# Spreading a norm weight by 128-row products, a reordered and fenced first stage, and tiles that start on multiples of 256 bytes

## The chip, the cores and the metric

The kernel runs on one core of one Trainium2 chip. The metric is the device time of one execution in microseconds (us), as the median of several runs. One execution was also recorded by the hardware profiler; its span runs from the first to the last instruction of the program.

## What is computed

One decoder layer on a sequence of 512 tokens with 1024 channels, all in 32-bit floats: a root-mean-square norm, one wide input projection, a gated linear recurrence (8 heads of 128, chunks of 32), causal multi-head attention with low-rank queries and keys (8 heads), a gated merge of the two branches, an output projection, a residual and a last norm. Cut to what matters:

```
h     = rms_norm(x, norm_g)                  # 512 x 1024
proj  = h @ w_in                             # 1024 x 7872 columns
hq, hf, hi, hz, cq, ckv, kr, mz, glog = split(proj)
y_a   = hgrn2_branch(hq, hf, hi, hz, ...)    # linear recurrence, silu gate
y_b   = mla_branch(cq, ckv, kr, mz, ...)     # causal attention, silu gate
gates = sigmoid(glog + b_gate)
x     = x + (gates[0] * (y_a @ w_proj_a) + gates[1] * (y_b @ w_proj_b)) @ w_out
out   = rms_norm(x, final_norm_g)
```

## The kernel before

Every large matrix product is made of three TensorE products. Each operand is split into a high part, which is the value rounded to the format fp32r, and a low part, which is the rest; `mm3` (L79 to L84) adds high by high (L82), high by low (L83) and low by high (L84) in one accumulator in PSUM. Weights come by DMA into one of three buffers `w_raw` of 128 x 1024 floats; `load_w` (L86 to L105; DMA at L100) casts them to `w_hi` on ScalarE (L103) and subtracts to get `w_lo` on VectorE (L104). There are four buffers of each.

**The first stage** (L145 to L302) norms the tokens, turns them so that channels lie on partitions (`hT`, a high and a low tile of 128 x 8 x 512), and makes the first 256 columns of the low-rank projection. It goes by four blocks of 128 tokens, t = 0 to 3. For each block: `squares` (L218) sums squares on ScalarE and takes the power -1/2 on GpSimd; `scaled` (L223) multiplies on VectorE the block by that and by the norm weight, which lies in two PSUM tiles `ng`, and writes `xn`; `turned` (L228) transposes eight pieces on TensorE (L233), copies them as `hT` high on ScalarE (L235) and subtracts to get `hT` low on VectorE (L236); `c_product` (L239) multiplies with the first two weight halves `c_raw` (L244), split by `c_split` (L212). Block 0 takes its own way to the root (L258 to L267), without GpSimd. The norm weight arrives as one row on one partition; two products with a row of ones (L254) spread it over 128 partitions. `idle_mm` (L207) makes products of a tile of zeros, whose result nobody reads.

**What sets the order.** The code of the first stage stands within `tc.manual_schedule` for TensorE, ScalarE and VectorE: their instructions keep the order in which they are written, among each other. All that is written after it is placed by a scheduler that goes by simulated times, and it may set later work in between. So products of the next 256 columns (L82 to L84 of `proj_tok`; their weights come through `load_cols`, L107) stand among those of the first stage, and so do the casts of their weights (L103). The SyncE queue issues nearly all DMAs in the written order.

**Where tiles lie.** Tiles get their places in SBUF one behind the other, from both ends of the memory. In the kernel before, tiles of 4 to 152 bytes a partition stand among the large ones. Added up, `w_raw`, `w_hi`, `w_lo`, `hT` and the output weights `wo` start 32 bytes past a multiple of 256 bytes; the two parts of `ya` and of `yb` (high and low of the branch outputs), `m` (merged) and `cT` (the low-rank rows, turned) start 224 bytes past one.

After the first stage come, in this order: the other columns of the low-rank projection, the recurrence in four pairs of heads with the input projection of each, attention head by head, the two merge projections, the output projection.

Of the kernel before, what the change touches and what calls it, by code (L numbers as in the profile page):

```python
# [38 lines left out]
def hybrid_layer(ctx: ExitStack, tc: tile.TileContext, a):  # L39
# [22 lines left out]
    class Pool:  # L62
# [5 lines left out]

        def tile(self, shape, dt, tag, bufs=1):
            return self.p.tile(shape, dt, tag=tag, name=tag, bufs=bufs)  # L70

        def close(self):
            self.cm.__exit__(None, None, None)

    hpool = Pool("hpool", "left")
    cpool = Pool("cpool", "right")
# [30 lines left out]
    def load_cols(mat, c0, w=256):  # L107

        v = mat[:, c0 : c0 + w].rearrange("(k p) c -> p k c", p=P)
        return [load_w(v[:, 4 * i : 4 * i + 4, :]) for i in range(2)]  # L110
# [13 lines left out]

    def proj_tok(mat, c0, w, lhs):

        halves = load_cols(mat, c0, w)
        ps = []
        for t2 in range(NT // 2):
            b = mm_tile()  # L130
            for t in range(2):
                tt = 2 * t2 + t
                for kk in range(KD):
                    mm3(b[:, t * 256 : t * 256 + w], lhs, halves[kk // 4],
                        (slice(None), kk, slice(tt * P, tt * P + P)), (slice(None), kk % 4),
                        kk == 0, kk == KD - 1)
            ps.append(b)
        return ps
# [6 lines left out]
    def power(out, x, mul, add, expo):  # L145

        nc.gpsimd.tensor_scalar(out, x, mul, add, op0=ALU.mult, op1=ALU.add)
        nc.gpsimd.tensor_tensor(out, out, expo, op=ALU.pow)
# [10 lines left out]
    ident = const.tile([P, P], F32, name="ident")  # L159
    neg_half = const.tile([P, 4], F32, name="neg_half")  # L160
    eps = const.tile([P, 1], F32, name="eps")
    nc.gpsimd.memset(eps[:], EPS)
    nc.gpsimd.memset(neg_half[:], -0.5)
    zero = st.tile([P, 512], BF16, "zero")
    ones = st.tile([1, P], F32, "ones")
    warm = st.tile([P, 1], F32, "warm")
    ng_row = st.tile([1, D], F32, "ng_row")
    x_sb = [st.tile([P, D], F32, "x", bufs=NT) for _ in range(NT)]
    hT = [hpool.tile([P, KD, S], F32R, f"hT{i}") for i in range(2)]
# [37 lines left out]
    def idle_mm(n):  # L207

        for _ in range(n):
            nc.tensor.matmul(idle[:], zero[:, :P], zero[:], start=True, stop=True)  # L210

    def c_split(kh, i, eng):  # L212

        hi, lo = c_hl[kh]
        nc.scalar.copy(hi[:, half[i]], c_raw[kh][:, half[i]])
        eng.tensor_tensor(lo[:, half[i]], c_raw[kh][:, half[i]], hi[:, half[i]].bitcast(F32), op=ALU.subtract)
# [31 lines left out]
    with tc.manual_schedule(engines={mybir.EngineType.PE, mybir.EngineType.Activation, mybir.EngineType.DVE}):  # L248
        nc.vector.memset(zero[:], 0.0)
        nc.vector.memset(ones[:], 1.0)  # L250
        nc.scalar.activation(warm[:], eps[:], AF.Sqrt)
        idle_mm(5)
        for n in range(2):
            nc.tensor.matmul(ng[n][:], ones[:], ng_row[:, half[n]], start=True, stop=True)  # L254
        idle_mm(3)

# [11 lines left out]
        scaled(0)  # L268
        c_split(0, 0, nc.vector)
        lo0 = turned(0, 0)  # L270
        lo0()
        c_split(0, 1, nc.vector)
        lo1 = turned(0, 1)
        c_product(0, 0, 0)
        c_product(0, 0, 1, (0, 1))
        c_product(0, 0, 2)
        c_product(0, 0, 1, (2, 3))
        lo1()
        squares(1)
        c_split(1, 0, nc.vector)  # L280
        c_split(1, 1, nc.gpsimd)
        squares(2)
# [5 lines left out]
        for t in range(1, NT):  # L288
            if t + 2 < NT:
                squares(t + 2)  # L290
            for kh in range(2):
                lo[kh]()
            if t + 1 < NT:
                scaled(t + 1)
            for kind in (0, 1, 2):
                c_product(t, 0, kind)
            if t + 1 < NT:
                nxt = [turned(t + 1, 0), turned(t + 1, 1)]
            for kind in (0, 2, 1):
                c_product(t, 1, kind)  # L300
            lo = nxt
    st.close()  # L302

# [33 lines left out]
    for c0, w in ((0, 256), (256, 256), (512, 192)):  # L337
        for t2, ps in enumerate(proj_tok(w_in, COL_C + c0, w, hT) if c0 else c_ps):
            nc.scalar.copy(c_sb[:, 2 * t2 : 2 * t2 + 2, c0 : c0 + w],
                           ps[:].rearrange("p (t c) -> p t c", t=2)[:, :, :w])  # L340
    css = cw.tile([P, 2, NT], F32, "css")
    for t in range(NT):
        for i, (o, n) in enumerate(((0, NQ), (NQ, NKV))):
            csq = cw.tile([P, NQ], F32, "csq", bufs=2)
            nc.scalar.activation(csq[:, :n], c_sb[:, t, o : o + n], AF.Square, accum_out=css[:, i, t : t + 1])
    power(css[:, 0, :], css[:, 0, :], 1.0 / NQ, EPS, neg_half[:])
    power(css[:, 1, :], css[:, 1, :], 1.0 / NKV, EPS, neg_half[:])
    kd = cw.tile([P, NT, 2, NR], F32, "kd")
# [126 lines left out]
    def hg_out(h, asb, st_, q128, v_sb):  # L475
# [8 lines left out]
        for i in range(NT):  # L484
            osq = W("osq", 1, (P, P))
            nc.scalar.activation(osq[:], ops[:, i * P : i * P + P], AF.Square, accum_out=ss[:, i : i + 1])
        power(ss[:], ss[:], 1.0 / P, 4 * EPS, neg_half[:])
        nc.vector.tensor_tensor(on[:].rearrange("p (g v) -> p g v", g=NT), ops[:].rearrange("p (g v) -> p g v", g=NT),
# [283 lines left out]
    m2p.close()  # L772
    mp.close()


# [36 lines left out]
```

## Time and profile before

| | us |
|---|---|
| median of 3 runs | 649.04 (648.63 to 650.54) |
| the profiled execution, its time | 648.64 |
| its span | 646.9 |
| TensorE busy (products) | 633.7, 98% |
| TensorE loading weights | 541.4, 84% |
| VectorE busy | 350.9, 54% |
| ScalarE busy | 240.7, 37% |
| GpSimd busy | 113.8, 18% |

PE is TensorE, PEld its weight loads, DVE is VectorE, ACT is ScalarE, POOL is GpSimd, SP is SyncE. A row of the timeline has the start, the duration, engine, line, operation, the tile written and the tiles read, and in brackets how long the engine was idle before it and what ended that. Products are pipelined and overlap, so the durations of single products don't add up; what one costs in a dense stretch is the distance from start to start. A row of the table of windows has the window, its length, busy time and count of instructions by engine, the granted TensorE clock as a share of full speed, the share of time in which the DMA engines were busy, and what they moved.

### The profile page before, as it was taken

How to read it: one execution, taken by the hardware profiler on the slowest of the kernel's cores; microseconds unless marked ns; L12 is line 12 of the kernel's file. 1: busy time of each engine (PE TensorE's matmuls, PEld its weight loads, DVE VectorE, ACT ScalarE, POOL GpSimd, SP SyncE). 2: the span in 40 equal slices, each digit the busy share in tenths (PEclk: the TensorE clock that was granted, in tenths of full speed). 3: DMA queues.
4: the chain of work that ended last, by engine and by line, in shares of the span. 5: the costliest groups of instructions: out<-in, count | busy, mean ns of one | idle time of the engine just before them, and what ended most of it. 6: DMA issues, size and time to landing. Idle time of an engine off the chain costs nothing.

```text
span 646.9 us, 9040 instructions
## 1 busy us (share of the span) xinstructions
PE 633.7 (98%) x3529; PEld 541.4 (84%) x3529; DVE 350.9 (54%) x543; ACT 240.7 (37%) x455; POOL 113.8 (18%) x212
## 2 busy tenths in 40 slices
PE   8799999999999999999999999999999999999995
PEld 4798988988898898888888988888888888888884
DVE  4533984676396377548485857845222342434244
ACT  5534422333223323435454546544122232323123
POOL 2104420331231032321223131000000010111011
PEclk9899999999999999999999999999999999999999
DMA  7433342142214113312424142133333323325403
GB/s 247 124 94 103 98 130 66 33 119 78 64 35 132 44 54 86 93 54 53 116 51 117 47 131 74 48 98 97 98 97 98 99 67 104 111 78 162 163 15 114
DMA packets 61944, 59.78 MB, mean 92 GB/s; under 512 B 5799, under 2 KB 57293, under 8 KB 61902
## 3 DMA queue, kind: packets, MB, share of 16 engines
q1 hardware_dynamic: 59628, 55.47, 29.1%
q10 hardware_dynamic: 2130, 3.22, 1.7%
q8 instruction: 27, 0.44, 0.3%
q0 software_dynamic: 144, 0.52, 0.3%
q14 instruction: 15, 0.12, 0.1%
HBM read 55.01 MB, written 2.10 MB: 88 GB/s over the span
## 4 chain that ended last, share of the span: by engine, by line
PE 96%; DMA 2%; SPq 0%; issue 0%; ACT 0%; DVE 0%; POOLq 0%; POOL 0%
PE mm_ps L82 26%; PE mm_ps L84 26%; PE mm_ps L83 26%; PE ax_ps L82 2%; PE ax_ps L83 2%; PE ax_ps L84 2%; PE ax_ps L604 2%; PE mm_ps L244 2%; DMA x<-x 1%; PE ax_ps L625 1%; PE ax_ps L461 1%; PE ax_ps L480 1%; PE ax_ps L482 1%; PE ax_ps L449 1%; DMA w_raw<-w_in 1%; PE ax_ps L469 1%
## 5 line engine op out<-in xcount | busy, mean ns | idle before, releaser
L104 DVE TENSOR_TENSOR w_lo<-w_raw,w_hi 128x1024 fp32r<-128x1024 f32 (+3 forms) x92 | 110.3, 1200 | 118.1 <-ACT w_hi L103 113.6
L103 ACT CAST w_hi<-w_raw 128x1024 fp32r<-128x1024 f32 (+3 forms) x92 | 89.8, 976 | 167.7 <-PE mm_ps L83 108.1
L82 PE MATMUL mm_ps<-hT,w_hi 128*128 128x512 f32 x384 | 151.5, 395 | 0.0
L84 PE MATMUL mm_ps<-hT,w_lo 128*128 128x512 f32 x384 | 150.5, 393 | 0.0
L83 PE MATMUL mm_ps<-hT,w_hi 128*128 128x512 f32 x384 | 150.0, 391 | 0.0
L84 PEld LDWEIGHTS mm_ps<-hT,w_lo 128*128 128x128 f32 x384 | 72.2, 188 | 14.9
L83 PEld LDWEIGHTS mm_ps<-hT,w_hi 128*128 128x128 f32 x384 | 72.2, 188 | 14.3
L82 PEld LDWEIGHTS mm_ps<-hT,w_hi 128*128 128x128 f32 x384 | 72.2, 188 | 14.2
L84 PE MATMUL mm_ps<-w_hi,hT 128*128 128x256 f32 (+1 forms) x192 | 54.3, 283 | 0.0
L82 PE MATMUL mm_ps<-w_hi,hT 128*128 128x256 f32 (+1 forms) x192 | 54.2, 282 | 0.0
L83 PE MATMUL mm_ps<-w_lo,hT 128*128 128x256 f32 (+1 forms) x192 | 54.1, 282 | 0.0
L715 POOL TENSOR_TENSOR ma<-ma,z 128x512 f32<-128x512 f32 x8 | 11.9, 1483 | 163.5 <-DVE z L714 163.5
L612 POOL TENSOR_SCALAR p<-p,sm 128x128 f32<-128x128 f32 (+3 forms) x32 | 20.3, 638 | 105.1 <-DVE sm L611 65.7
L82 PEld LDWEIGHTS mm_ps<-w_hi,hT 128*128 128x128 f32 x192 | 36.6, 191 | 0.2
L83 PEld LDWEIGHTS mm_ps<-w_lo,hT 128*128 128x128 f32 x192 | 36.6, 190 | 0.2
L84 PEld LDWEIGHTS mm_ps<-w_hi,hT 128*128 128x128 f32 x192 | 36.6, 190 | 0.0
L406 DVE RECIPROCAL tf<-pr 128x512 f32<-128x512 f32 x8 | 26.8, 3350 | 0.2
L610 ACT ACTIVATE p<-ax_ps,sm 128x128 f32<-128x128 f32 (+3 forms) x32 | 16.8, 528 | 23.2 <-DVE sm L609 22.9
L82 PE MATMUL mm_ps<-ya,w_hi 128*128 128x512 f32 x64 | 25.3, 396 | 0.0
L83 PE MATMUL mm_ps<-ya,w_hi 128*128 128x512 f32 x64 | 25.3, 395 | 0.0
L84 PE MATMUL mm_ps<-ya,w_lo 128*128 128x512 f32 x64 | 25.3, 395 | 0.0
L83 PE MATMUL mm_ps<-yb,w_hi 128*128 128x512 f32 x64 | 25.2, 394 | 0.0
(218 smaller groups left out, 1143.8 us busy)
## 6 DMA issues: line engine op xcount, KB each, us to landing
w_raw<-w_in SPq DMA_DIRECT2D x60, 512.0 KB, 4.0
w_raw<-w_proj_a SPq DMA_DIRECT2D x8, 512.0 KB, 3.7
w_raw<-w_proj_b SPq DMA_DIRECT2D x8, 512.0 KB, 3.5
wo_raw<-w_out SPq DMA_DIRECT2D x8, 512.0 KB, 3.3
w_raw<-w_ukv SPq DMA_DIRECT2D x16, 128.0 KB, 2.5
xr<-x SPq DMA_DIRECT2D x4, 512.0 KB, 6.5
x<-x SPq DMA_DIRECT2D x3, 512.0 KB, 8.9
w_raw<-w_uq SPq DMA_DIRECT2D x8, 192.0 KB, 2.8
```

The costliest lines, as they stand in the source:

```text
L82: nc.tensor.matmul(ps, lh[lsl], rh[rsl], start=start, stop=False)
L83: nc.tensor.matmul(ps, lh[lsl], rl[rsl], start=False, stop=False)
L84: nc.tensor.matmul(ps, ll[lsl], rh[rsl], start=False, stop=stop)
L103: nc.scalar.copy(hi[:, :o], raw[:, :o])
L104: (lo_eng or nc.vector).tensor_tensor(lo[:, :o], raw[:, :o], hi[:, :o].bitcast(F32), op=ALU.subtract)
L244: nc.tensor.matmul(ps, hT[l][:, 4 * kh + k, t * P : t * P + P], c_hl[kh][r][:, k * 256 : k * 256 + 256], start=kh == 0 and kind == 0 and k ...
L406: nc.vector.reciprocal(rp[:], pr[:])
L449: nc.tensor.matmul(sps[:, sl], kt_[:, sl], v_sb[:, i, (h % 2) * P : (h % 2) * P + P], start=True, stop=True)
L604: nc.tensor.matmul(sps[:, :n], qh[:, bl], kpe[x][:, :n], start=False, stop=x == 1)
L610: nc.scalar.activation(p[:, :n], sps[:, :n], AF.Exp, scale=SCALE, bias=sm[:, 1:2], accum_out=sm[:, 2:3])
L612: nc.gpsimd.tensor_scalar(p[:, :n], p[:, :n], sm[:, 3:4], 0.5, op0=ALU.mult, op1=ALU.mult)
L715: nc.gpsimd.tensor_tensor(ma[:, j], ma[:, j], g[:], op=ALU.add)
```

## The change

1. The norm weight. Two tiles `ng_r` of 128 x 1024 are cleared (a memset of a float tile and two casts, since fp32r is written by a cast); the first row of one gets the high part of the norm weight, that of the other the low part. Four fp32r products with a 128 x 128 tile of ones (high for both halves, then low) replace the two float products on one row.
2. The split of the first weights. Their high halves for block 0 are cast on VectorE in place of ScalarE, the low halves are made on VectorE and GpSimd; both transposes of block 0 stand ahead of its first product; the products of block 0 follow the order high-high, low-high, high-low without being split in two. The idle products become 6, 3, 3, 2 and 4 in number, from 5 and 3.
3. `tc.no_sync_barrier()` behind the first stage: nothing written after it is placed ahead of anything written before it. It makes no engine wait. The loads and splits of the next 256 columns are now written within the stage, after block 3 has been turned, and handed to `proj_tok`.
4. `Pool.tile` rounds each tile of these pools up to a multiple of 256 bytes a partition, a pool `edge` of 224 bytes is set at the right end, and `eps` and `neg_half` share a tile. Every tile of the pools, and each weight buffer, then starts on a multiple of 256 bytes.

```
         def tile(self, shape, dt, tag, bufs=1):
+            n = int(np.prod(shape[1:]))
+            q = 256 // mybir.dt.size(dt)
+            if n % q:
+                wide = self.p.tile([shape[0], -(-n // q) * q], dt, tag=tag, name=tag, bufs=bufs)[:, :n]
+                return wide if len(shape) == 2 else wide.rearrange("p (a b) -> p a b", a=shape[1])
             return self.p.tile(shape, dt, tag=tag, name=tag, bufs=bufs)
+    edge = Pool("edge", "right")
+    edge.p.tile([P, 56], F32, name="edge")
...
-    def proj_tok(mat, c0, w, lhs):
+    def proj_tok(mat, c0, w, lhs, halves=None):
-        halves = load_cols(mat, c0, w)
+        halves = halves or load_cols(mat, c0, w)
...
-    neg_half = const.tile([P, 4], F32, name="neg_half")
-    eps = const.tile([P, 1], F32, name="eps")
+    fixed = const.tile([P, 5], F32, name="fixed")
+    neg_half, eps = fixed[:, 0:4], fixed[:, 4:5]
-    ones = st.tile([1, P], F32, "ones")
+    ones = st.tile([P, P], F32, "ones")
+    ones_r = st.tile([P, P], F32R, "ones_r")
+    ng_z = st.tile([P, D], F32, "ng_z")
+    ng_r = [st.tile([P, D], F32R, f"ng_r{i}") for i in range(2)]
...
-    def c_split(kh, i, eng):
+    def c_hi(kh, i, eng):
+        eng(c_hl[kh][0][:, half[i]], c_raw[kh][:, half[i]])
+    def c_lo(kh, i, eng):
         hi, lo = c_hl[kh]
-        nc.scalar.copy(hi[:, half[i]], c_raw[kh][:, half[i]])
         eng.tensor_tensor(lo[:, half[i]], c_raw[kh][:, half[i]], hi[:, half[i]].bitcast(F32), op=ALU.subtract)
...
-        nc.scalar.activation(warm[:], eps[:], AF.Sqrt)
-        idle_mm(5)
-        for n in range(2):
-            nc.tensor.matmul(ng[n][:], ones[:], ng_row[:, half[n]], start=True, stop=True)
-        idle_mm(3)
+        nc.vector.tensor_copy(ones_r[:], ones[:])
+        nc.vector.memset(ng_z[:], 0.0)
+        for i in range(2):
+            nc.vector.tensor_copy(ng_r[i][:], ng_z[:])
+        nc.scalar.activation(warm[:], eps, AF.Sqrt)
+        idle_mm(6)
+        nc.vector.tensor_copy(ng_r[0][0:1], ng_row[:])
+        nc.vector.tensor_tensor(ng_r[1][0:1], ng_row[:], ng_r[0][0:1].bitcast(F32), op=ALU.subtract)
+        for x in range(2):
+            for n in range(2):
+                nc.tensor.matmul(ng[n][:], ones_r[:], ng_r[x][:, half[n]], start=x == 0, stop=x == 1)
+            idle_mm(3)
...
         scaled(0)
-        c_split(0, 0, nc.vector)
-        lo0 = turned(0, 0)
+        lo0, lo1 = turned(0, 0), turned(0, 1)
+        for i in range(2):
+            c_hi(0, i, nc.vector.tensor_copy)
         lo0()
-        c_split(0, 1, nc.vector)
-        lo1 = turned(0, 1)
+        c_lo(0, 0, nc.vector)
+        c_lo(0, 1, nc.gpsimd)
+        lo1()
+        idle_mm(2)
         c_product(0, 0, 0)
-        c_product(0, 0, 1, (0, 1))
         c_product(0, 0, 2)
-        c_product(0, 0, 1, (2, 3))
-        lo1()
+        c_product(0, 0, 1)
+        idle_mm(4)
         squares(1)
-        c_split(1, 0, nc.vector)
-        c_split(1, 1, nc.gpsimd)
+        for i in range(2):
+            c_hi(1, i, nc.scalar.copy)
+        c_lo(1, 0, nc.vector)
+        c_lo(1, 1, nc.gpsimd)
...
             if t + 1 < NT:
                 scaled(t + 1)
+            else:
+                c_second = load_cols(w_in, COL_C + 256)
...
             lo = nxt
+    tc.no_sync_barrier()
     st.close()
...
-        for t2, ps in enumerate(proj_tok(w_in, COL_C + c0, w, hT) if c0 else c_ps):
+        for t2, ps in enumerate(proj_tok(w_in, COL_C + c0, w, hT, c_second if c0 == 256 else None) if c0 else c_ps):
```

How the change moves instructions, at three places. In the rows below stand the line, the operation, the tile written, the tiles read, the size written, and xN where N alike follow each other; `hT` with the lower number is the high part. Lines of the kernel after are shifted: its L111 is L103 of before, its L247 L235, L256 L244, L90 to L92 are L82 to L84.

First, ScalarE from block 0's copies to those of block 2, before: two casts of `w_hi` at L103, which belong to the next 256 columns, stand ahead of the copies of `hT` for block 1.

```order
L215 CAST w_hi<-w_raw 128x512
L235 CAST hT_112<-ax_ps 128x4x128
L215 CAST w_hi<-w_raw 128x512
L235 CAST hT_112<-ax_ps 128x4x128
L220 ACTIVATE sq,rs<-x 128x1024
L215 CAST w_hi<-w_raw 128x512 x2
L220 ACTIVATE sq,rs<-x 128x1024
L103 CAST w_hi<-w_raw 128x1024 x2
L235 CAST hT_112<-ax_ps 128x4x128 x2
L220 ACTIVATE sq,rs<-x 128x1024
L235 CAST hT_112<-ax_ps 128x4x128 x2
```

The same place after:

```order
L247 CAST hT_119<-ax_ps 128x4x128 x2
L232 ACTIVATE sq,rs<-x 128x1024
L224 CAST w_hi<-w_raw 128x512 x2
L232 ACTIVATE sq,rs<-x 128x1024
L247 CAST hT_119<-ax_ps 128x4x128 x2
L232 ACTIVATE sq,rs<-x 128x1024
L247 CAST hT_119<-ax_ps 128x4x128 x4
L111 CAST w_hi<-w_raw 128x1024 x2
```

The two casts of the next columns have moved behind all copies of `hT`, and the two casts of the first weights for block 0 have left ScalarE.

Second, VectorE at the start, before, up to the first instruction that waits for a sum of squares:

```order
L249 MEMSET zero 128x256
L250 MEMSET ones 1x128
L261 TENSOR_SCALAR rsq_165<-rs 128x1
L263 TENSOR_SCALAR rsq_167<-rs,rsq_165 128x1
L264 TENSOR_SCALAR rsq_167<-rsq_167 128x1
```

And after:

```order
L261 MEMSET zero 128x256
L262 MEMSET ones 128x128
L263 CAST ones_r<-ones 128x128
L264 MEMSET ng_z 128x1024
L266 CAST ng_r_113<-ng_z 128x1024
L266 CAST ng_r_114<-ng_z 128x1024
L270 CAST ng_r_113<-ng_row 1x1024
L271 TENSOR_TENSOR ng_r_114<-ng_row,ng_r_113 1x1024
L281 TENSOR_SCALAR rsq_184<-rs 128x1
```

Six instructions now stand ahead of the root of block 0, two of which wait for the row of the norm weight. Further on, the two VectorE instructions on the masks (L317 and L318 before), which stood ahead of the low part of the second weight half, stand behind the whole stage.

Third, TensorE near the end of the stage, before: products of the next columns (L82 to L84) and the transpose of small parameters (L307) stand among the transposes and products of the stage.

```order
L233 MATMUL ax_ps<-ident,xn 128x128 x4
L82 MATMUL mm_ps<-w_hi,hT_112 128x256
L83 MATMUL mm_ps<-w_lo,hT_112 128x256
L233 MATMUL ax_ps<-ident,xn 128x128 x4
L244 MATMUL mm_ps<-w_hi,hT_112 128x256 x4
L244 MATMUL mm_ps<-w_hi,hT_113 128x256 x4
L244 MATMUL mm_ps<-w_lo,hT_112 128x256 x4
L307 MATMUL ax_ps<-ident,rows 128x38
L84 MATMUL mm_ps<-w_hi,hT_113 128x256
```

And after, where the stage ends:

```order
L256 MATMUL mm_ps<-w_hi,hT_119 128x256 x4
L256 MATMUL mm_ps<-w_hi,hT_120 128x256 x4
L256 MATMUL mm_ps<-w_lo,hT_119 128x256 x4
L334 MATMUL ax_ps<-ident,rows 128x38
L90 MATMUL mm_ps<-w_hi,hT_119 128x256
L91 MATMUL mm_ps<-w_lo,hT_119 128x256
L92 MATMUL mm_ps<-w_hi,hT_120 128x256
```

Nothing of the next columns is left within the stage: 24 products that stood between its transposes and products now follow it. From there on the order is that of before on every engine.

More of the change, by code (lines that the diff above doesn't have):

```diff
@@ L159, in hybrid_layer @@
     ident = const.tile([P, P], F32, name="ident")
-    neg_half = const.tile([P, 4], F32, name="neg_half")
-    eps = const.tile([P, 1], F32, name="eps")
-    nc.gpsimd.memset(eps[:], EPS)
-    nc.gpsimd.memset(neg_half[:], -0.5)
+    fixed = const.tile([P, 5], F32, name="fixed")
+    neg_half, eps = fixed[:, 0:4], fixed[:, 4:5]
+    nc.gpsimd.memset(eps, EPS)
+    nc.gpsimd.memset(neg_half, -0.5)
     zero = st.tile([P, 512], BF16, "zero")
-    ones = st.tile([1, P], F32, "ones")
+    ones = st.tile([P, P], F32, "ones")
+    ones_r = st.tile([P, P], F32R, "ones_r")
     warm = st.tile([P, 1], F32, "warm")
     ng_row = st.tile([1, D], F32, "ng_row")
+    ng_z = st.tile([P, D], F32, "ng_z")
+    ng_r = [st.tile([P, D], F32R, f"ng_r{i}") for i in range(2)]
     x_sb = [st.tile([P, D], F32, "x", bufs=NT) for _ in range(NT)]
@@ L345, in hybrid_layer @@
             nc.scalar.activation(csq[:, :n], c_sb[:, t, o : o + n], AF.Square, accum_out=css[:, i, t : t + 1])
-    power(css[:, 0, :], css[:, 0, :], 1.0 / NQ, EPS, neg_half[:])
-    power(css[:, 1, :], css[:, 1, :], 1.0 / NKV, EPS, neg_half[:])
+    power(css[:, 0, :], css[:, 0, :], 1.0 / NQ, EPS, neg_half)
+    power(css[:, 1, :], css[:, 1, :], 1.0 / NKV, EPS, neg_half)
     kd = cw.tile([P, NT, 2, NR], F32, "kd")
@@ L486, in hg_out @@
             nc.scalar.activation(osq[:], ops[:, i * P : i * P + P], AF.Square, accum_out=ss[:, i : i + 1])
-        power(ss[:], ss[:], 1.0 / P, 4 * EPS, neg_half[:])
+        power(ss[:], ss[:], 1.0 / P, 4 * EPS, neg_half)
         nc.vector.tensor_tensor(on[:].rearrange("p (g v) -> p g v", g=NT), ops[:].rearrange("p (g v) -> p g v", g=NT),
@@ L773, in hybrid_layer @@
     mp.close()
+    edge.close()
 _INS = ["x", "norm_g", "w_in", "b_gate", "lb_logits", "hg_norm_g", "q_a_g", "w_uq", "kv_a_g", "w_ukv",
```

## The prediction

> **What bounds the kernel now.** I read the page first, its shares, its clock row and its chain of waits.
>
> ```profile
> span 646.9 us, 9040 instructions
> PE 633.7 (98%) x3529; PEld 541.4 (84%) x3529; DVE 350.9 (54%) x543; ACT 240.7 (37%) x455; POOL 113.8 (18%) x212
> PEclk9899999999999999999999999999999999999999
> PE 96%; DMA 2%; SPq 0%; issue 0%; ACT 0%; DVE 0%; POOLq 0%; POOL 0%
> ```
>
> TensorE is the bound: 98% busy, 96% of the chain. So the time can fall in two ways only: TensorE waits less or runs at a higher clock (the second digit of the clock row, 16 to 32 us, is an 8), or each product takes less. I ask the first in the opening, the second in the dense rest. First the timeline from 12 to 27 us, on ACT, DVE and PE:
>
> ```profile
> 13.96 0.63 DVE L317 COPY mask_inf<-maskf 128x128 f32<-128x128 f32 x1 [1.97 <-DMA maskf<-c_masks]
> 14.65 0.68 DVE L216 TENSOR_TENSOR w_lo<-w_raw,w_hi 128x512 fp32r<-128x512 f32 x1
> 13.22 1.29 POOL L216 TENSOR_TENSOR w_lo<-w_raw,w_hi 128x512 fp32r<-128x512 f32 x1 [0.18 <-ACT w_hi L215]
> 15.38 0.74 PE L244 MATMUL mm_ps<-w_lo,hT 128*128 128x256 f32 x4 [1.21 <-DVE w_lo L216]
> 16.13 1.29 PE L233 MATMUL ax_ps<-ident,xn 128*128 128x128 f32 x8
> 17.60 1.04 ACT L103 CAST w_hi<-w_raw 128x1024 fp32r<-128x1024 f32 x1 [3.41 <-DMA w_raw<-w_in]
> 19.10 1.04 ACT L103 CAST w_hi<-w_raw 128x1024 fp32r<-128x1024 f32 x1 [0.46 <-DMA w_raw<-w_in]
> 20.05 1.06 ACT L235 CAST hT<-ax_ps 128x512 fp32r<-128x512 f32 x2
> 20.68 1.22 PE L244 MATMUL mm_ps<-w_hi,hT 128*128 128x256 f32 x4 [3.26 <-ACT hT L235]
> 21.70 1.06 PE L244 MATMUL mm_ps<-w_lo,hT 128*128 128x256 f32 x4
> 22.55 1.05 PE L244 MATMUL mm_ps<-w_hi,hT 128*128 128x256 f32 x4
> ```
>
> TensorE has turned block 1 by 17.42 (16.13 + 1.29) and then stands for 3.26 us. It waits for the copy of `hT`, which stands on ScalarE behind two casts of weights that the DMA has not brought yet. When it goes on, four products take 0.85 us (21.70 to 22.55): 213 ns each. The table of windows has the reason, and the prices in the dense part:
>
> ```profile
> 17.50:20.60 3.10, 0.00 (x0) 0.00 (x0) 1.65 (x2) 2.54 (x4) 0.00 (x0) 0.98 0.60 186
> 20.70:23.80 3.10, 3.10 (x14) 3.04 (x15) 3.10 (x5) 1.46 (x3) 1.47 (x5) 0.50 0.73 165
> 123.50:134.99 11.49, 11.49 (x97) 11.49 (x96) 9.94 (x10) 3.15 (x4) 5.02 (x21) 1.00 0.18 48
> 440.27:451.18 10.91, 10.91 (x49) 9.01 (x48) 4.41 (x5) 2.77 (x3) 0.00 (x0) 1.00 0.47 137
> 451.20:462.38 11.18, 11.18 (x49) 8.99 (x48) 3.14 (x3) 2.71 (x4) 0.00 (x0) 1.00 0.35 101
> 618.00:625.50 7.50, 7.50 (x34) 6.09 (x33) 1.66 (x2) 0.65 (x1) 0.00 (x0) 1.00 0.00 0
> ```
>
> After the idle window the granted clock is 0.50, so the pause costs twice. In the dense windows the count holds one product that began before, so starts are one fewer: 256-column products with `hT` cost 11.49 / 96 = 120 ns; 512-column products with `hT` 10.91 / 48 = 227 ns; with `ya` 11.18 / 48 = 233 ns; with `m` and `wo` 7.50 / 32 or 33, 227 to 234, and by single starts 233. At full clock twice the half-clock speed would be 106 ns for 256 columns and 213 for 512. So each product pays 14 to 20 ns beyond the columns, and which of the two goes with the tiles and not with traffic: the `hT` window moved 137 GB/s, the dearer `ya` window 101, and the last none.
>
> **Part 1, the pause.** The fence and the new place of the casts put the copies of `hT` for block 1 right behind the transposes. The pause of 3.26 goes. What is late next is the copy itself, 0.53 us behind its transposes (half of 1.06), and the second half of the transposes covers it. −3.2 us.
>
> **Part 2, the clock.** The twelve products from 20.68 to 23.4 cost 213 in place of 120 ns: 12 x 0.093 = 1.1; some four of the transposes behind them were slow too, at about twice 0.11: 0.4. −1.5 us, provided no new pause is as long.
>
> **Part 3, the masks.** DVE waited for the masks until 13.96 and only then made the low half that the product at 15.38 waited for. Now masks come behind the stage; the other half, on GpSimd, is done at 13.22 + 1.29 = 14.51 and is late next. −0.8 us.
>
> **Part 4, the opening.** Rows:
>
> ```profile
> 0.85 0.27 DVE L249 MEMSET zero<- 128x256 uint32 x1 [0.85 <-PEq L803]
> 1.08 0.17 DVE L250 MEMSET ones<- 1x128 f32 x1
> 3.42 3.78 PE L254 MATMUL ax_ps<-ng_row,ones 1*128 1x512 f32 x4
> 5.49 0.29 ACT L262 ACTIVATE rsq<-rs,rsq 128x1 f32<-128x1 f32 x1
> 6.64 1.41 DVE L225 SCALAR_TENSOR_TENSOR xn<-x,rs,ax_ps 128x512 f32<-128x512 f32 x2
> 9.96 0.62 ACT L215 CAST w_hi<-w_raw 128x512 fp32r<-128x512 f32 x1
> 18.68 1.23 DVE L104 TENSOR_TENSOR w_lo<-w_raw,w_hi 128x1024 fp32r<-128x1024 f32 x1 [2.03 <-ACT w_hi L103]
> ```
>
> The 3.78 us of row products were hidden: `xn` began at 6.64, when the root was there, and its halves ran back to back. Removing them gains nothing. New is the DVE list ahead of the root: a cast of 128 columns (0.2, as the memset of that size), a memset of 1024 (four times 0.27: 1.1), three casts of 1024, and a subtraction at 1.23. The trace has no SBUF cast of 1024 on DVE; at dearest it costs the subtraction's 1.23, at cheapest half of it. Two of the list need the norm weight's row, and the root's steps queue behind them; the row was there by 3.42, when its products began. From 1.25 the list ends at 5.6 to 7.5. From the start of ACT's root to `xn` takes 6.64 − 5.49 = 1.15, and one small DVE step ahead of it 0.2, so `xn` starts at 6.95 to 8.85: 0.3 to 2.2 us late. I take 0.6, near the cheap end, since copies have half the operands. Against that, the cast of 0.62 at 9.96 leaves ACT, where it delayed the second copy of `hT`. The four new products and the idle ones run while TensorE waits anyway. DVE takes two casts of `w_hi` instead, hidden behind the transposes, and GpSimd one more low half (1.29) ahead of block 1's root, while ACT still sums that block's squares. Net 0, from −0.6 to +1.6.
>
> **Part 5, what the fence takes.** In the loop over blocks TensorE now has no foreign products to fill waits: a block waits for subtract, scale and copy in turn. One chain per block: low half 0.7, scale 0.7 for the first half, four transposes 0.45, copy 0.55, against 12 products of 1.44 and eight transposes of 0.9. That leaves some 0.3 to 0.4 us open in two blocks: +0.7 (0 to 1.5). The casts of the next columns end after block 3's copies: two casts of 1.04 and two subtractions of 1.23 behind each other take 1.04 + 2 x 1.23 = 3.5 us from the last copy; the 24 products of block 3 last 2.9, and the second half is needed 12 products later. Cover is there by about 1 us; without it, up to +1.2. SyncE's next loads wait for these buffers and come some 6 us later; the 96 products of those columns, 11.5 us, hide them.
>
> In the chain in order of time the stage's last products are
>
> ```profile
> 33.12 2.88 PE mm_ps L244 x24
> ```
>
> so it ends at 36.0, with 24 foreign products of 120 ns among its own: 33.1 without them.
>
> The first stage sums to −3.2 − 1.5 − 0.8 + 0 + 0.7 = −4.8 us.
>
> **Part 6, the tile starts.** Counts, from the groups by line and shape:
>
> ```profile
> L82 PE MATMUL mm_ps<-hT,w_hi 128*128 128x512 f32 x384 | 151.5, 395 | 0.0
> L82 PE MATMUL mm_ps<-w_hi,hT 128*128 128x256 f32 (+1 forms) x192 | 54.2, 282 | 0.0
> L82 PE MATMUL mm_ps<-ya,w_hi 128*128 128x512 f32 x64 | 25.3, 396 | 0.0
> L83 PE MATMUL mm_ps<-yb,w_hi 128*128 128x512 f32 x64 | 25.2, 394 | 0.0
> L82 PE MATMUL mm_ps<-cT,w_hi 128*128 128x512 f32 x52 | 20.8, 401 | 0.0
> L82 PE MATMUL ax_ps<-wo,m 128*128 128x512 f32 x40 | 15.9, 398 | 0.0
> L83 PE MATMUL mm_ps<-wo,m 128*128 128x512 f32 x24 | 9.5, 398 | 0.0
> ```
>
> Each stands three times (L82, L83, L84): 1152 products with `hT` at 227 ns; 3 x (64 + 64 + 52 + 40 + 24) = 732 of the dear kind at 233 (`cT` taken as such); and about 580 of 256 columns at 120 (160 in each line, the other 32 having 192 columns, and the 96 of the stage). The cheap kind has both tiles 32 bytes past a multiple of 256 (and so of 128), the dear kind has one 224 past (96 past a multiple of 128). That start and price go together is what I infer; no product in this trace starts both tiles on a multiple of 64. The nearest rows give the ends. If only the difference between kinds goes: 732 x 0.0062 = −4.5 us. If all that lies beyond the columns goes: 1152 x 0.014 + 732 x 0.020 + 580 x 0.014 = −39 us. Between them a straight line through the two prices: 64 bytes nearer to the 128-byte mark saves 6.2 ns, the last 32 would save 3.1. Then 1152 x 0.0031 + 732 x 0.0093 + 580 x 0.0031 = 3.6 + 6.8 + 1.8: −12.2 us, my value, since it keeps to both rows. Upwards, if 0 past is a dearer start, the price of the dear kind for all: 1152 x 0.0062 + 580 x 0.0031 = +8.9.
>
> [...]
>
> **Sum.** 648.64 is the profiled execution's time, 1.7 over its span; the median is 0.4 above. −4.8 − 12.2 = −17.0 on the profiled execution gives 631.6, and on the median 632.0.
>
> **Rivals.**
> The tile starts do nothing to TensorE: the two prices come from something else that goes with the tiles. For it: no aligned product is in the trace. Then 649.0 − 4.8 = 644.2. A neighbour, only the dear kind becomes cheap, 639.7, I count to the forecast.
> All of the extra goes: 649.0 − 4.8 − 39 = 605. [...] Against: a single step of 64 bytes moved only 6.2 of 20 ns.
> Slower: with every tile on the same low address bits, the weight load of one product and the columns of another meet in the same place, and every product takes the dear price: +8.9 − 4.8 = 653.1. It decides from 4.2 ns on each `hT` product, 231.3 ns. Against: `hT` and `w_hi` share their low bits already and are the cheap pair.
> No gain left: tile starts do nothing and the stage's gain is eaten, by the DVE list at its dear end (+1.6), the cover of the casts gone (+1.2) and waits in the loop at 1.5 in place of 0.7: −4.8 + 3.6 = −1.2, 647.8.
>
> **Chances.** Forecast, part 6 worth 3 to 30 us: 0.45. All goes: 0.15. Starts do nothing: 0.24. No gain left: 0.06. Slower: 0.10. The likeliest gives 632. About 0.3% (2 us) is what a measurement of this kernel tells from no change: faster 0.84, same 0.06, slower 0.10. The range from 606 to 646 leaves out the slower case, most of no gain, and a little below.
>
> **What the profile after would show.** Part 1: no wait on TensorE over 1 us behind block 1's transposes; wrong if `hT` still comes late. Part 2: granted clock 1.00 from 20 to 24 us. Part 3: the masks behind the stage. Part 4: `xn` starts near 7.2; over 8.5 the casts are dear. Part 5: the stage's last product ends near 28 (33.1 less 4.8). Part 6 is decided by three windows: 512-column products with `hT` and with `ya` at 224 ns, 256-column ones at 117. [...] What would make all wrong is a new pause of some microseconds in the dense part, where the order is as before.

## The result and the profile after

The changed kernel takes 638.65 us (median of 4 runs, 638.63 to 639.33); the kernel before, beside it, 649.27 (4 runs, 648.63 to 650.54). The ratio is 0.9837, with a 95% interval of 0.9820 to 0.9854: some 10.6 us, 1.6%, faster. The forecast was 632.0, with a range from 606 to 646. The direction and the range held; the time is 6.6 us above the forecast.

The profiled execution took 638.65. Its page, the rows that answer to those of before:

```profile
span 636.9 us, 9069 instructions
PE 627.3 (99%) x3539; PEld 540.1 (85%) x3539; DVE 353.9 (56%) x550; ACT 239.4 (38%) x453; POOL 115.4 (18%) x213
PEclk9999999999999999999999999999999999999998
PE 97%; DVE 1%; ACT 0%; issue 0%; POOLq 0%; POOL 0%
```

TensorE is still the bound. The 8 in the clock row, between 16 and 32 us, is gone (the new one at the end lies behind the last product, which starts at 629.61: the granted clock is 1.00 from 23.80 to 630 and 0.50 from 634.00 on). To see where the 10 us of span went, one marker is enough: the first product of 192 columns, which stands at the same place in both programs, and the last product of all. Timeline of before, then of after:

```profile
44.48 0.26 PE L82 MATMUL mm_ps<-w_hi,hT 128*128 128x192 f32 x1
...
639.56 0.39 PE L84 MATMUL ax_ps<-wo,m 128*128 128x512 f32 x1
```

```profile
38.91 0.25 PE L90 MATMUL mm_ps<-w_hi,hT 128*128 128x192 f32 x1
...
629.61 0.39 PE L92 MATMUL ax_ps<-wo,m 128*128 128x512 f32 x1
```

Up to the marker 44.48 − 38.91 = 5.6 us are gained: that is the first stage. From the marker to the end it is 595.1 before and 590.7 after: 4.4 us, the dense part. The stretch behind the marker hardly varies: in the changed kernel and in the seven kernels below whose weights and streams lie alike it takes 590.70 to 590.72. So both parts of the forecast can be read by themselves.

**The first stage.** Timeline of after, TensorE, ScalarE and VectorE (the lines of before plus 12: L256 is the stage's product, L245 the transpose, L247 the copy of `hT`, L111 and L112 the split of the next columns, L344 the first mask):

```profile
14.02 0.64 PE L256 MATMUL mm_ps<-w_lo,hT 128*128 128x256 f32 x4
14.50 1.03 PE L245 MATMUL ax_ps<-ident,xn 128*128 128x128 f32 x8
15.14 1.07 ACT L247 CAST hT<-ax_ps 128x512 fp32r<-128x512 f32 x2 [1.63 <-PE ax_ps L245]
15.77 0.74 PE L256 MATMUL mm_ps<-w_hi,hT 128*128 128x256 f32 x4 [0.24 <-ACT hT L247]
16.35 0.64 PE L256 MATMUL mm_ps<-w_lo,hT 128*128 128x256 f32 x4
16.83 0.64 PE L256 MATMUL mm_ps<-w_hi,hT 128*128 128x256 f32 x4
17.84 1.29 PE L245 MATMUL ax_ps<-ident,xn 128*128 128x128 f32 x8 [0.37 <-DVE xn L237]
23.44 2.01 ACT L111 CAST w_hi<-w_raw 128x1024 fp32r<-128x1024 f32 x2
24.53 2.36 DVE L112 TENSOR_TENSOR w_lo<-w_raw,w_hi 128x1024 fp32r<-128x1024 f32 x2
26.55 0.64 PE L256 MATMUL mm_ps<-w_lo,hT 128*128 128x256 f32 x4
26.81 0.22 DVE L344 COPY mask_inf<-maskf 128x128 f32<-128x128 f32 x1
27.30 0.39 PE L90 MATMUL mm_ps<-w_hi,hT 128*128 128x256 f32 x1
```

The pause of 3.26 us is now 0.24: the copy of `hT` starts as soon as four transposes are there, since the casts of the next columns stand at 23.44. Four products take 0.48 (16.35 to 16.83), the full-clock price, where before they took 0.85. The last low products of block 0 go at 14.02 without a wait, at 15.38 before. The masks come behind the stage. What is left are waits of 0.24 and 0.37, one or none in a block. The stage's last product ends at 27.19 (26.55 + 0.64), against 36.0 before, of which 2.9 were foreign.

**The dense part.** The table of windows of after, at the places of the four dense windows of before (256 columns with `hT`; 512 with `hT`; 512 with `ya`; 512 with `m`); again each count holds one product that began earlier:

```profile
117.97:129.48 11.51, 11.51 (x97) 11.51 (x96) 9.95 (x10) 3.14 (x4) 5.05 (x21) 1.00 0.16 47
433.99:444.87 10.88, 10.88 (x49) 9.01 (x48) 4.54 (x5) 2.78 (x3) 0.00 (x0) 1.00 0.46 138
444.87:455.75 10.88, 10.88 (x49) 9.01 (x48) 3.14 (x3) 2.71 (x4) 0.00 (x0) 1.00 0.37 104
606.03:613.51 7.48, 7.48 (x34) 6.19 (x33) 1.23 (x1) 1.05 (x1) 0.00 (x0) 1.00 0.00 0
```

Products with `hT` stay at 227 ns (10.88 / 48) and 120 (11.51 / 96). Those with `ya` fell from 233 to the same 227, and so did those with `m` (7.48 / 33). Nothing went below 227. So only the difference between the two kinds is gone. At 6.6 ns (233.3 to 226.7 over whole runs of 48 starts) 732 products make 4.8 us; the 96 products of 256 columns with `cT` went the other way, from 117 to 120, and take back 0.3. The marker gives 4.4. The forecast gave this part 12.2.

### The profile page after: what moved, and what is told of

The parts are those of the page before. It is cut to its first block, busy times and chain, and to the rows that moved or that the text cites. A ratio compares the mean times of both kernels' runs of the same rounds, so it can differ in the third digit from the quotient of the medians.

```text
span 636.9 us, 9069 instructions
## 1 busy us (share of the span) xinstructions
PE 627.3 (99%) x3539; PEld 540.1 (85%) x3539; DVE 353.9 (56%) x550; ACT 239.4 (38%) x453; POOL 115.4 (18%) x213
## 4 chain that ended last, share of the span: by engine, by line
PE 97%; DVE 1%; ACT 0%; issue 0%; POOLq 0%; POOL 0%
PE mm_ps L90 26%; PE mm_ps L92 26%; PE mm_ps L91 26%; PE ax_ps L91 2%; PE ax_ps L90 2%; PE ax_ps L92 2%; PE ax_ps L631 2%; PE mm_ps L256 1%; PE ax_ps L652 1%; PE ax_ps L488 1%; PE ax_ps L507 1%; PE ax_ps L509 1%; PE ax_ps L476 1%; PE ax_ps L496 1%; PE ax_ps L493 1%; PE ax_ps L523 1%
## 5 line engine op out<-in xcount | busy, mean ns | idle before, releaser
L112 DVE TENSOR_TENSOR w_lo<-w_raw,w_hi 128x1024 fp32r<-128x1024 f32 (+3 forms) x92 | 109.0, 1186 | 114.5 <-ACT w_hi L111 110.0
L90 PE MATMUL mm_ps<-hT,w_hi 128*128 128x512 f32 x384 | 151.3, 394 | 0.0
L111 ACT CAST w_hi<-w_raw 128x1024 fp32r<-128x1024 f32 (+3 forms) x92 | 89.8, 977 | 163.0 <-PE mm_ps L91 110.6
L92 PE MATMUL mm_ps<-hT,w_lo 128*128 128x512 f32 x384 | 150.2, 392 | 0.0
L92 PEld LDWEIGHTS mm_ps<-hT,w_lo 128*128 128x128 f32 x384 | 72.1, 188 | 14.8
L90 PEld LDWEIGHTS mm_ps<-hT,w_hi 128*128 128x128 f32 x384 | 72.2, 188 | 14.1
L92 PE MATMUL mm_ps<-w_hi,hT 128*128 128x256 f32 (+1 forms) x192 | 54.1, 282 | 0.0
L90 PE MATMUL mm_ps<-w_hi,hT 128*128 128x256 f32 (+1 forms) x192 | 54.0, 282 | 0.0
L90 PEld LDWEIGHTS mm_ps<-w_hi,hT 128*128 128x128 f32 x192 | 36.4, 190 | 0.2
L92 PEld LDWEIGHTS mm_ps<-w_hi,hT 128*128 128x128 f32 x192 | 36.5, 190 | 0.0
L90 PE MATMUL mm_ps<-ya,w_hi 128*128 128x512 f32 x64 | 25.0, 390 | 0.0
L92 PE MATMUL mm_ps<-ya,w_lo 128*128 128x512 f32 x64 | 24.9, 389 | 0.0
L92 PE MATMUL mm_ps<-yb,w_lo 128*128 128x512 f32 x64 | 24.9, 389 | 0.0
```

The costliest lines, as they stand in the source:

```text
L90: nc.tensor.matmul(ps, lh[lsl], rh[rsl], start=start, stop=False)
L92: nc.tensor.matmul(ps, ll[lsl], rh[rsl], start=False, stop=stop)
L111: nc.scalar.copy(hi[:, :o], raw[:, :o])
L112: (lo_eng or nc.vector).tensor_tensor(lo[:, :o], raw[:, :o], hi[:, :o].bitcast(F32), op=ALU.subtract)
```

## Experiments: what the tile starts do

Two theories can give these prices. In the one, each tile pays for its own place: a start 0 or 32 bytes past a multiple of 128 is cheap, one 96 bytes past it is dear. In the other, the difference counts: a product is cheap when the tile that is loaded and the tile that streams start at the same place modulo some power of two. Before, `hT` and the weights were both 32 past a multiple of 256, and `ya` was 192 bytes apart from them.

**The starts alone.** The kernel before with part 4 of the change and nothing else:

```
+            n = int(np.prod(shape[1:]))
+            q = 256 // mybir.dt.size(dt)
+            if n % q:
...
+    edge.p.tile([P, 56], F32, name="edge")
...
+    fixed = const.tile([P, 5], F32, name="fixed")
```

> The kernel before with the tile starts alone changed (rounded tiles, edge pool, shared small tile); the first stage as before. Two theories of the product price. Theory D (difference): the price of a 512-column product goes by the distance between the starts of its two tiles, 0 apart 227 ns, 192 bytes apart 233 ns. Theory S (own start): it goes by each tile's own distance past a multiple of 128, 0 or 32 past cheap, 96 past dear. Both expect here 227 ns for hT, ya, yb and m, so 732 x 6.6 ns = 4.8 us less than before: 644.4. If the whole gain of the change were 10.6 and the stage gives the rest, the stage is worth 5.8. A third view, that the starts do nothing, expects 649.3.

Measured: 643.97 (642.85 to 644.37), ratio 0.9913 [0.9898, 0.9927]. By the median of the distances from start to start, the 512-column products of every tile cost 227. From the marker to the end it is 590.7, as in the changed kernel. The pause and the half clock are still there (lines of this kernel, +7 against before):

```profile
19.31 1.23 PE L251 MATMUL mm_ps<-w_hi,hT 128*128 128x256 f32 x4 [3.10 <-ACT hT L242]
20.33 1.05 PE L251 MATMUL mm_ps<-w_lo,hT 128*128 128x256 f32 x4
21.18 1.06 PE L251 MATMUL mm_ps<-w_hi,hT 128*128 128x256 f32 x4
```

The copy that ends the pause stands behind this cast on ScalarE, which waits for its weights:

```profile
17.73 1.04 ACT L110 CAST w_hi<-w_raw 128x1024 fp32r<-128x1024 f32 x1 [0.37 <-DMA w_raw<-w_in]
```

Beside it the kernel before had 649.50, so the kernel gains 5.5 us by the medians. Only the 4.4 from the marker on belong to the products. The marker itself came 1.4 us earlier than in the trace of before (43.10 for 44.48), by the same 1.4 as the cast above (17.73 for 19.10), since SyncE issued the weight loads from 12.13 on in place of 13.32. In the six kernels that share the changed first stage (the changed one and five below) these loads start between 12.66 and 13.46, so the place varies from trace to trace; that the new starts moved it is not shown. The three parts on the first stage are worth 643.97 − 638.65 = 5.3 by the medians, and 43.10 − 38.91 = 4.2 by the markers of the two traces; the trace of the starts alone is the fastest of its six runs (642.85).

**All tiles moved by the same 96 bytes.** The changed kernel, with all tiles 96 bytes past a multiple of 256, the dear place of the first theory, but all alike:

```
-    edge.p.tile([P, 56], F32, name="edge")
+    edge.p.tile([P, 32], F32, name="edge")
...
+    const.tile([P, 24], F32, name="pad")
     ident = const.tile([P, P], F32, name="ident")
```

> The kernel after with every tile moved by 96 bytes, on both sides of the memory, so that all start 96 past a multiple of 256 and the distance between any two is as in the kernel after. Theory D: products stay at 227 and 120 ns, time as the kernel after, 638.7. Theory S: all 1152 + 732 products of 512 columns go to 233 ns, 1884 x 6.6 ns = 12.4 us, time 651.

Measured: 639.14 (638.69 to 639.54), ratio 0.9840 [0.9819, 0.9860], and in the windows

```profile
118.54:130.06 11.52, 11.52 (x98) 11.52 (x96) 9.96 (x10) 3.15 (x4) 5.06 (x21) 1.00 0.17 47
434.58:445.46 10.88, 10.88 (x49) 9.01 (x48) 4.54 (x5) 2.77 (x3) 0.00 (x0) 1.00 0.48 142
445.46:456.34 10.88, 10.88 (x49) 9.01 (x48) 3.14 (x3) 2.72 (x4) 0.00 (x0) 1.00 0.35 99
```

120, 227 and 227 ns: as if nothing had been moved. Multiples of 256 bytes are not what helps. The theory of each tile's own place falls.

**Other distances.** The changed kernel again, `hT` left in its place, with `cT`, `ya`, `m` and `yb` moved against their weights by four distances in each of two kernels. The first, for 192, 160, 128 and 96 bytes (the second has 40, 8, 8 and 16 elements in these four lines, for 64, 32, 32 and 224):

```
-    edge.p.tile([P, 56], F32, name="edge")
+    edge.p.tile([P, 8], F32, name="edge")
+    yap.p.tile([P, 8], F32, name="pad_ya")
+    m2p.p.tile([P, 16], F32, name="pad_m")
+    ybsp.p.tile([P, 8], F32, name="pad_yb")
```

> The kernel after with the tiles of the right side moved against those of the left: cT by 192 bytes, ya by 160, m by 128, yb by 96; weights, hT and wo stay. Theory D: cT at 233 ns per 512-column product and 117 per 256-column product as before the change, and each of the other distances has a price of its own, above 227 unless the distance is a whole period. Theory S: cT (64 past 128), ya (32 past) and m (0 past) stay at 227, only yb (96 past) is at 233.

> The same with other distances: cT by 64 bytes, ya by 32, m by 32, yb by 224 (or 32 the other way). Theory D: prices go by distance; if the direction does not count, ya and yb are alike. Theory S: cT, ya and m at 227, yb (96 past 128) at 233. In both hT stays at 227.

Measured: 643.35 and 642.37, one run each. By the median of single starts, `cT` 192 apart 233 ns, `ya` 160 apart 234, `m` 128 apart 232, `yb` 96 apart 232; in the second kernel `cT` 64 apart 230, `ya` 32 apart 234, `m` 32 apart 232, `yb` 224 apart 235. The products with `hT` stay at 227 in both. The windows of the first (`hT`, `ya`, `yb`) and of the second (`ya`, `yb`):

```profile
434.89:445.78 10.89, 10.89 (x49) 9.01 (x48) 4.37 (x5) 2.76 (x3) 0.00 (x0) 1.00 0.47 141
445.78:457.02 11.24, 11.24 (x49) 9.04 (x48) 3.14 (x3) 2.72 (x4) 0.00 (x0) 1.00 0.36 98
512.28:523.49 11.21, 11.21 (x49) 9.02 (x48) 3.14 (x3) 3.15 (x4) 1.30 (x1) 1.00 0.34 94
```

```profile
444.85:456.06 11.21, 11.21 (x50) 9.00 (x49) 3.14 (x3) 2.72 (x4) 0.00 (x0) 1.00 0.35 104
511.21:522.42 11.21, 11.21 (x50) 9.02 (x49) 3.14 (x3) 3.17 (x4) 1.29 (x1) 1.00 0.33 95
```

Each window has 48 distances from start to start: 233 to 234 ns. In all, the price is 230 to 235 at the seven distances from 32 to 224 bytes and 227 at none; it does not grow with the distance.

**Every pair apart.** The hard test is whether `hT`, cheap in all kernels so far, can be made dear:

```
-    edge.p.tile([P, 56], F32, name="edge")
+    edge.p.tile([P, 32], F32, name="edge")
...
+    hpool.p.tile([P, 24], F32, name="pad_h")
     hT = [hpool.tile([P, KD, S], F32R, f"hT{i}") for i in range(2)]
```

> The changed kernel with every tile that is multiplied with a weight tile (hT, ya, yb, cT, and the merged m against wo) moved 96 bytes, the weight tiles left where they are: in all 1,884 products of 512 columns the two tiles now start 96 bytes apart. Theory 'difference of the two starts': all of them cost 231 to 235 ns, the products with hT too, which were cheap in every kernel so far, and those of 256 columns 117 to 118 in place of 120. 1,884 x 6 ns less 576 x 2.5 ns: +9.9 us, 648.5 (645 to 651). Rival 'hT is cheap for another reason' (its shape, its order in memory, its place in the stage): 227 for hT as before, only the 732 others dear, 643.0.

Measured: 648.90 (10 runs, 648.36 to 649.64), ratio to before 0.9999 [0.9988, 1.0009].

```profile
119.10:130.49 11.39, 11.39 (x97) 11.39 (x96) 9.82 (x10) 3.16 (x4) 4.94 (x20) 1.00 0.17 47
438.68:449.88 11.20, 11.20 (x49) 9.01 (x48) 4.40 (x5) 2.76 (x3) 0.00 (x0) 1.00 0.48 137
449.88:461.08 11.20, 11.20 (x49) 9.01 (x48) 3.14 (x3) 2.71 (x4) 0.00 (x0) 1.00 0.33 98
```

`hT` is dear now: 11.20 / 48 = 233 ns. From its marker (39.22) to its last product (640.22) this kernel takes 601.0, 10.3 more than the changed one. By the window prices it would be 1,884 x 6.6 ns less 576 x 1.3 = 11.7; so the average product loses a little less than those in the windows. Ninety-six bytes between the weights and all that they are multiplied with cost about as much as the whole change brings. The products of 256 columns go the other way, 11.39 / 96 = 118.7 in place of 120.

**The period.** `ya` and `m` 256 bytes apart, `yb` 512:

```
+    yap.p.tile([P, 64], F32, name="pad_ya")
+    m2p.p.tile([P, 64], F32, name="pad_m")
+    ybsp.p.tile([P, 64], F32, name="pad_yb")
```

> The changed kernel with ya and m moved by 256 bytes against their weights, and yb by 512; hT and cT stay. Theory 'only the address within 256 bytes counts': all 512-column products stay at 227, 638.7 to 639.3. Rival 'the address within 512 bytes counts': ya and m at 231 to 235, yb at 227; 384 x 6 ns = +2.3, about 641. Rival 'the tiles must lie a certain way however far apart': yb dear as well, 642.5.

Measured: 639.26 in one run; windows of `hT`, `ya` and `yb`:

```profile
434.61:445.49 10.88, 10.88 (x49) 9.01 (x48) 4.54 (x5) 2.78 (x3) 0.00 (x0) 1.00 0.46 142
445.49:456.37 10.88, 10.88 (x49) 9.01 (x48) 3.14 (x3) 2.71 (x4) 0.00 (x0) 1.00 0.35 99
510.77:521.65 10.88, 10.88 (x49) 9.01 (x48) 3.14 (x3) 3.08 (x4) 1.29 (x1) 1.00 0.35 96
```

All 227: a distance of 256 is as good as none. The changed kernel's rule, every tile on a multiple of 256, is one way to keep all pairs alike.

## Experiments: what the first stage is made of

**The fence and the later casts, without the rest.** The kernel with the starts alone, plus part 3 of the change; opening and split as before:

```
+            else:
+                c_second = load_cols(w_in, COL_C + 256)
...
+    tc.no_sync_barrier()
     st.close()
```

> The kernel before with the new tile starts, the fence and the later casts of the next columns; the opening (norm weight on one row) and the split of the first weights as before. The starts alone gave 643.97, the whole change 638.65, so 5.3 us are left to share out. Theory 'the pause': the 3.26 us wait behind block 1's transposes and the slow clock after it go with the fence and the later casts, the rest stays: about 4 of the 5.3, so 640.0 (639.4 to 640.6), and the first product of block 1 follows its transposes by under 0.6 us. Rival 'all parts needed': without the new opening and split another wait takes the place of the pause, 641.5 to 643. Rival 'nothing but the fence': 638.7, opening and split are worth nothing.

Measured: 639.07 (5 runs, 639.06 to 639.32), ratio 0.9838 [0.9824, 0.9852]. TensorE, in its lines:

```profile
14.57 0.51 PE L251 MATMUL mm_ps<-w_lo,hT 128*128 128x256 f32 x2 [0.16 <-POOL w_lo L223]
14.92 1.03 PE L240 MATMUL ax_ps<-ident,xn 128*128 128x128 f32 x8
16.19 0.74 PE L251 MATMUL mm_ps<-w_hi,hT 128*128 128x256 f32 x4 [0.24 <-ACT hT L242]
```

The pause is 0.24 here too. Of the 5.3 us that the starts left over, 4.9 come with these few lines; by the markers, 43.10 and 39.33, it is 3.8 of 4.2. By the medians that is more than the 4 that the first theory gave them, and the time is below its range; the third, that opening and split are worth nothing, is nearer.

**The fence alone taken out.** The casts stay in their later place, by the hand order:

```
-    tc.no_sync_barrier()
     st.close()
```

> The changed kernel without the fence alone; the casts of the next columns stay in their later place, since the hand order puts them there. The copies of the masks go back ahead of the low half on VectorE. Theory 'the place of the casts': the pause stays away without a fence, only the masks cost, so block 0's low products start about 0.8 us later and the time is 639.3 (638.7 to 639.9). Rival 'the fence itself': casts of later weights come ahead of block 1's copies of hT again and the pause of about 3 us with them, 642 to 643. Second rival: products of later stages fill the waits of this one, so it is a little faster than with the fence, 637.9.

Measured: 640.19 (639.25 to 640.68), ratio 0.9854 [0.9838, 0.9869]. VectorE, then TensorE:

```profile
13.94 0.53 DVE L343 COPY mask_inf<-maskf 128x128 f32<-128x128 f32 x1 [1.56 <-DMA maskf<-c_masks]
14.39 0.21 DVE L344 CAST mask_le<-maskf 128x128 uint8<-128x128 f32 x1
14.53 0.68 DVE L228 TENSOR_TENSOR w_lo<-w_raw,w_hi 128x512 fp32r<-128x512 f32 x1
```

```profile
15.26 0.74 PE L256 MATMUL mm_ps<-w_lo,hT 128*128 128x256 f32 x4 [0.87 <-DVE w_lo L228]
16.01 1.28 PE L245 MATMUL ax_ps<-ident,xn 128*128 128x128 f32 x8
17.32 0.75 PE L256 MATMUL mm_ps<-w_hi,hT 128*128 128x256 f32 x4
```

The masks are back ahead of the low half, and the products behind it start at 15.26 in place of 14.02; the loss stays to the marker (40.51 in place of 38.91). No pause comes behind block 1's transposes. So the place of the casts takes the pause away. The fence is worth 1.5 us by the medians here, above the 0.7 (up to 1.3) of the first theory and outside its range, and far from the 3 to 4 of the rival. By the traces most of it is the masks. Of the 1.6 us at the marker, 0.2 are there before them: the eight products ahead begin at 13.09 in place of 12.88, with the full clock granted at 9.41 in place of 8.27. What the masks cost hangs on when their DMA lands. It landed for 13.94 here; in the trace of the starts alone the masks were copied at 12.67, also ahead of the low half, and the first low products followed at 14.02 without a wait. The four runs without the fence spread from 639.25 to 640.68.

**The norm weight as before,** on one row, and **the first split as before,** both in the changed kernel:

```
-        for x in range(2):
-            for n in range(2):
-                nc.tensor.matmul(ng[n][:], ones_r[:], ng_r[x][:, half[n]], ...)
+        for n in range(2):
+            nc.tensor.matmul(ng[n][:], ones[:], ng_row[:, half[n]], start=True, stop=True)
```

> The changed kernel with the norm weight spread as before (two float products on one row, 5 and 3 idle products); everything else as changed. The VectorE list of memsets and casts ahead of the root goes. Theory 'neutral': xn starts earlier (6.6 in place of 7.56 us), but the clock of the transposes decides, 638.65 within 0.5. Rival 'xn decides': the new products made xn 0.9 us late, so the time is 637.6 to 638.0. Rival 'the clock': the four long row products load TensorE less than the new ones, the clock comes later and the time is 639.5 to 640.5.

```
-        lo0, lo1 = turned(0, 0), turned(0, 1)
-        for i in range(2):
-            c_hi(0, i, nc.vector.tensor_copy)
-        lo0()
-        c_lo(0, 0, nc.vector)
-        c_lo(0, 1, nc.gpsimd)
+        c_hi(0, 0, nc.scalar.copy)
+        c_lo(0, 0, nc.vector)
+        lo0 = turned(0, 0)
+        lo0()
+        c_hi(0, 1, nc.scalar.copy)
+        c_lo(0, 1, nc.vector)
+        lo1 = turned(0, 1)
         lo1()
```

> The changed kernel with the first 512-row half of block weights split as before: both high halves on ScalarE between the copies of hT, both low halves on VectorE. Theory: the second copy of hT of block 0 comes about 0.6 us later and the low half of the second 512 columns no earlier than on GpSimd; TensorE waits for one of them, 639.0 (638.7 to 639.5). Rival: the split on two engines was worth nothing, 638.65 within 0.3. Rival: it was the larger part of the 1.3 us beside the pause, 639.7 to 640.

Measured: 639.29 (639.01 to 639.72) and 639.13 (638.26 to 639.74), ratios 0.9842 [0.9828, 0.9856] and 0.9838 [0.9823, 0.9853]; the changed kernel has 638.65 (638.63 to 639.33). Each lies 0.5 to 0.6 higher, and the spreads overlap. What goes with this half microsecond is seen in the traces: the time at which the full clock is granted. It was granted at 4.45 us in the trace of the old split, 8.27 in that of the changed kernel, 11.46 in that with one row and 11.84 in that with fence and casts alone, and the marker follows in this order: 38.43, 38.91, 39.33, 39.33. The six kernels with the changed first stage rise with the clock in the same way: granted at 4.59, 8.27, 8.88, 9.95, 10.14 and 10.15, the marker stands at 38.44, 38.91, 38.93, 39.22, 39.48 and 39.51. With the clock at 4.59 the new split has its marker at 38.44, with the clock at 4.45 the old one has it at 38.43: at an equal clock the split is worth nothing in these two traces, and the forecast of 639.0 for the old split, a wait of some half a microsecond, came true by number only. With the norm weight on one row `xn` starts at 7.26, not at the 6.6 that was expected, and the marker stands no later than with the new spreading at a like clock (39.33 against 39.51). So neither the new spreading nor the new split is shown to be worth anything. No kernel of the study has a lower median than the changed one.

## Why the prediction was right, and where it was wrong

**Part 1, the pause, −3.2:** right. 3.26 became 0.24, by the place of the casts, as the runs with and without the fence show; what is late next is the copy itself, as said.

**Part 2, the clock, −1.5:** right. The granted clock is 1.00 from 17.50 to 23.80, where it was 0.50 from 20.70 on; four products take 0.48 in place of 0.85. In the kernel with the starts alone pause and half clock stay together: 3.10 of pause, then four products in 0.85 (20.33 to 21.18).

**Part 3, the masks, −0.8:** right in place; the size is not fixed. The low products start 1.36 earlier, with clock and split changed as well, and taking the fence out cost 1.5, most of it by the masks; where their DMA landed earlier, at 12.67, they cost the first low products no wait.

**Part 4, the opening, 0:** right on the whole, with one wait unforeseen. In the profile after

```profile
2.63 1.29 DVE L266 CAST ng_r<-ng_z 128x1024 fp32r<-128x1024 f32 x2
4.55 1.21 DVE L271 TENSOR_TENSOR ng_r<-ng_row,ng_r 1x1024 fp32r<-1x1024 f32 x1
6.54 1.41 PE L274 MATMUL ax_ps<-ng_r,ones_r 128*128 128x512 f32 x2
7.56 1.41 DVE L237 SCALAR_TENSOR_TENSOR xn<-x,rs,ax_ps 128x512 f32<-128x512 f32 x2 [0.59 <-PE ax_ps L274]
```

the casts take 0.65 each, the cheap end, and the list ends at 5.76, near the forecast's early end of 5.6. `xn` starts at 7.56 in place of 7.2 all the same, since it waits 0.59 for the low products of the norm weight, which run behind three idle ones that take 1.50 (from 5.59). The forecast counted these products as hidden. In the run with the old split, where the full clock was granted at 4.45, the three idle ones take 0.82 (from 5.14) and `xn` starts at 7.08. No run shows that this cost time: with one row `xn` is earlier (7.26) and the marker is not.

**Part 5, the fence's price, +0.7:** right. Two waits on the loop, 0.24 and 0.37. The casts end at 26.89 (24.53 + 2.36), 0.4 ahead of the products at 27.30: covered, though not by the full microsecond.

The stage came to −5.6 by the marker, for −4.8 forecast, and to −4.2 by the marker (−5.3 by the medians) against the kernel with the starts alone. Some of this is the clock of the one trace: with the markers of all six kernels that have the changed stage, 38.44 to 39.51, the −5.6 would be −6.0 to −5.0.

**Part 6, the tile starts, −12.2:** wrong in size. The step that failed is the straight line through the two prices, "64 bytes nearer to the 128-byte mark saves 6.2 ns, the last 32 would save 3.1". It gave each product a price by how far its tiles lie from a mark. The run with all tiles moved by 96 bytes shows that this distance has no price. What counts is whether the two tiles of a product lie alike: 227 ns at 0, 256 and 512 bytes apart, 230 to 235 at the seven distances tried from 32 to 224. `hT` and the weights were alike before, so 1,152 products had nothing to gain. That the part gained at all was luck as far as the straight line goes: it asked for starts near a mark, and the change happened to set all tiles alike. The right size stood in the prediction as the lower end, "only the difference between kinds goes", −4.5, with 639.7 as its time; the marker shows −4.4. The trace of before would have allowed either reading, since its cheap pairs were alike and near the mark at once; the sentence that `hT` and `w_hi` share their low bits and are the cheap pair stood in the working against the slower rival, and was not carried over to the value. With −4.4 for −12.2 (+7.8), and a stage better by 0.8, the profiled execution would have been forecast at 638.6; it took 638.65.

The place of the one tile against the other changes the price by 6.6 ns in 227, with the same work on the other engines: in the windows with `ya` of the changed kernel and of the one with every pair apart, 3.14 us on VectorE and 2.71 on ScalarE in both, and 9.01 of weight loads. The runs show this dependence on the difference alone, and not its cause. Nor do they show which loaded tile counts, the product's own or that of the next product, whose load stands beside the running product in the trace (434.00 and 433.99 in that of after): in each dense stretch both start alike.

What the remaining 14 ns of each product are (227 less 213, which 256 columns cost at half clock, four in 0.85 us, and which is taken here for 512 at full clock) stays open. That the price at half clock holds nothing beyond the columns, which the rival "all of the extra goes" leaned on, is taken for granted in that 213 and shown by no run. No start or distance tried went below 227.

## What to carry to other kernels

When two kinds of the same product differ by a few per cent in a dense stretch, compare where their two tiles lie against each other, modulo 256 bytes, before looking at traffic; here tiles of 4 to 152 bytes among the large ones had set them 192 bytes apart, at 233 in place of 227 ns. Before extrapolating from two prices, list what else differs between the two rows: here "near a mark" and "alike" fell together, and one pad that moves all tiles alike separates them. In a hand-ordered stage, look first for foreign instructions that a scheduler has set in front of a copy that TensorE waits for: keeping two casts and two mask copies behind it was worth 3.8 us by the markers (4.9 by the medians), about as much as the 4.4 of 732 cheaper products.

## What the runs showed of the hardware that was not expected

- A product of fp32r tiles with 512 columns cost 227 ns when the two tiles started alike modulo 256 bytes (as the change sets them, and with `ya` and `m` moved by 256 and `yb` by 512), and 230 to 235 when they started 32, 64, 96, 128, 160, 192 or 224 bytes apart.
- With 256 columns it was the other way: 120 when alike, 117 to 119 when apart (`cT` 192 bytes apart in the kernel before 117, `hT` 96 apart 118.7).
- The time of the first full clock varied from 4.45 to 11.93 us over these kernels, among those with the changed opening from 4.45 to 10.15, and the end of the first stage came later with it: by 1.1 us, from 38.44 to 39.51 at the marker, among kernels with one and the same stage whose clock came at 4.59 to 10.15.
- When a load landed varied between traces with the same order on the queue. SyncE came to the weight loads at 12.13 in the trace of the starts alone and at 13.32 in that of before, and the masks let VectorE go on at 12.67 and at 13.96. The 1.4 us by which the marker of the starts alone is early lie there and not in the products.
